# Gate units of the memory branch between its last tile groups, and the heads' sums of squares made by ScalarE, in a hybrid encoder layer on one core

## The chip, the core and the metric

The kernel runs on one core of one Trainium2 chip (trn2). The core has a matrix engine (TensorE, PE in the rows, whose weight loads are listed apart as PEld), a vector engine (VectorE, DVE), a scalar engine for activation functions (ScalarE, ACT), GpSimd (POOL), and SyncE (SP), which here issues all transfers between HBM and on-chip memory. Each engine executes its own instructions in the order in which the program has them, and waits on semaphores for the others. The metric is the device time of one execution in microseconds.

## What is computed

One layer of a streaming encoder, for 1024 prompt rows and 32 sample rows of width 1024, in float32. From the normalised input one projection makes the inputs of three branches: differential attention with 4 heads, a linear recurrence (LRU), and cross-attention into 256 memory tokens with 4 heads of 64. Each branch has a SiLU gate. The gated results are concatenated, projected and added to the input. What the change touches of it:

```python
# memory branch
qm = rms_norm(mq.reshape(B, T, MX_HEADS, MX_HEAD_DIM), p['mx_q_norm_g'])
sm = jnp.einsum('bqhd,bkhd->bhqk', qm, m_k.astype(qm.dtype)).astype(f32) * (MX_HEAD_DIM ** -0.5)
pm = jax.nn.softmax(sm, axis=-1)
om = jnp.einsum('bhqk,bkhd->bqhd', pm.astype(qm.dtype), m_v.astype(qm.dtype)).reshape(B, T, MX_WIDTH)
out_c = om * jax.nn.silu(mg)
# attention branch: every head's output has its own norm
o = rms_norm(o, p['da_subln_g']) * (1.0 - lambda_init)
out_a = o.reshape(B, T, DA_WIDTH) * jax.nn.silu(dg)
y = x + jnp.concatenate([out_a, out_b, out_c], axis=-1) @ p['w_out']
```

## The kernel before

**Precision.** TensorE multiplies in a reduced float32 format (`F32R`). Each operand is split into a high and a low part (`XH`, `XL` of the normalised input, `WH`, `WL` of the weights), and a product is three matmuls (`mm3`, lines 607 to 609: high by high, high by low, low by high). A tile is split by ScalarE, which copies it into the high part, and VectorE, which subtracts (`split`, lines 436 and 438). Weights are split so by `split_all` (lines 591 and 593) into a ring of 4480 columns. A chunk gets its place in the ring only when the unit that last used the old contents there is through (`gone`).

**Units.** The row tiles are 8 of 128 prompt rows and one of 32 sample rows (index 8, `NT`). A unit is one PSUM bank of a projection: `unit_nat` (line 607 and, for the sample rows, 629) makes a row tile by 256 or 384 columns with 24 matmuls (16 for the sample rows), `unit_T` makes 128 features by 352 rows with 24 matmuls of 352 columns. The units of the projections run in the order of `ORDER`: head 0, LRU input, LRU gate, head 1, first half of the attention's gate, memory keys and values (`mk`, `mv`), memory queries with their gate (`mq`, `mg`), heads 2 and 3, second half of the attention's gate (`dg1`), and then the output projection (`wo`) in four blocks of 256 columns.

**The memory branch.** `mem_q` goes through five groups of tiles, four of two full tiles and the sample rows. A tile's unit makes its queries. `mem_probs` norms them, transposes them (L1235), makes the scores in two halves of two heads (L1254, L1256), takes the maximum (DVE, L1260) and the exponential with its sum (ACT, L1263, into `mw`). `mem_pt` divides by the sum (POOL, L1271, `mw`), transposes (PE, L1277), and splits into `PT`; `mem_out` multiplies with the values (L1301). Between groups, `mem_q` puts units of the gate `mg`: there are six (two blocks of 128 features by three blocks of 352 rows), each followed on ACT by a tanh (L971) and on DVE by a product (L972), `silu2`. `paced(mg)` issues one unit if one is left; `unpaced(mg)` issues what is left after the last group.

**The mixing.** The attention's output goes through HBM (`o_d`, with a 129th column per head that carries the epsilon of its norm). For each tile, `mix_T` multiplies the other two branches by their gates (POOL, L1170) and splits them into `XH`, `XL` (rows 4 to 7), and `mix_diff` does the attention's part: load `mn`, square (ACT, L1205), sum per head (DVE, L1206), power -1/2 (POOL, L447, `mrs`), scale (POOL, L1209), transpose (PE, L1214), multiply by gain and gate (DVE, L1215, `mg`), split into rows 0 to 3 of `XH`, `XL`. It can start when the attention of head 2 is done, while head 3's still runs. An output unit multiplies rows 4 to 7 first and then rows 0 to 3 (`ks = [4, 5, 6, 7, 0, 1, 2, 3]`), so its second half waits for `mix_diff`.

**What orders the instructions.** A list scheduler in the file (`Sched`) runs when the kernel is built. The functions above are generators that yield one instruction each, with its engine, a cost and what it depends on; the scheduler always issues the one that can start earliest by those costs, and among those that can start within a window the one of the best priority (`PR`). Nothing is reordered on the chip. A change of any cost or of the order of the units can therefore move instructions on every engine.

Of the kernel before, what the change touches and what calls it, by code (L numbers as in the profile page):

```python
# [9 lines left out]
AF = mybir.ActivationFunctionType  # L10
ALU = mybir.AluOpType
AX = mybir.AxisListType
# [25 lines left out]

PR = {"att": 6, "consts": 37, "evac": 11, "fetch": 1, "fetch0": 11, "gate": 53, "kq": 27, "lru": 13, "lrus": 58, "lrux": 48, "memc": 33, "meme": 47, "memo": 19, "memp": 48, "mempt": 55, "mems": 3, "mixT": 53, "mixd": 22, "normT": 16, "normT0": 34, "out": 16, "outin": 34, "silu": 18, "split": 56, "split0": 56}

TUNE = {"LAG": 0, "O": 3, "PENALTY": 1283, "S": 6, "acc": 3, "aging": 12, "lanes": 3, "tr": 4, "wACT": 455, "wDVE": 94, "wPE": 11, "wPOOL": 54, "F": 1.07, "M": 200, "twice": 127, "LAG2": 3}
LEAST = {"acc": 2, "tr": 1, "S": 2, "O": 1}

PE, ACT, DVE, POOL, SP = "PE", "ACT", "DVE", "POOL", "SP"
# [191 lines left out]
def c_act(n, ap=0, acc=False, sb=False):  # L236
    return (90.0 if sb else 51.0) + 0.833 * n + 93.0 * ap + (93.0 if acc else 0.0)


def c_dve(n, ap=0, fast=False):  # L240
    return 68.0 + (0.52 if fast else 1.042) * n + 60.0 * ap
# [14 lines left out]
def emit(tc, A, Y):  # L256
    nc = tc.nc
    V_, S_, G_, T_, Q_ = nc.vector, nc.scalar, nc.gpsimd, nc.tensor, nc.sync
# [922 lines left out]
    def mix_diff(i):  # L1181
        n, t0 = rows_of(i), i * P
        d = yield WAIT, mix_up
# [9 lines left out]
        g = yield GET, mn_s  # L1193
        mn = mixp.t([P, 4, P + 1], "mn", bufs=2)
        if n < P:
            g = yield from clear(mn, 516, [g])
        d = yield from dma(mn[:n], o_d[t0:t0 + n], od + [g], kb=258)
# [3 lines left out]
        g = yield GET, msq_s  # L1201
        msq = mixp.t([P, 4, P + 1], "msq")
        mss = mixp.t([P, 4], "mss", bufs=2)
        mrs = mixp.t([P, 4], "mrs", bufs=2)
        d = yield ACT, c_act(516, sb=True), [d, g], lambda: S_.activation(out=msq[:n], in_=mn[:n], func=AF.Square)  # L1205
        d = yield DVE, c_dve(516), [d], lambda: V_.tensor_reduce(out=mss[:n], in_=msq[:n], axis=AX.X, op=ALU.add)  # L1206
        msq_s.rel(d)
        d = yield from rsqrt(mrs, mss, n, 4, [d])
        d = yield POOL, c_pool(512), [d], lambda: G_.tensor_tensor(  # L1209
            out=mn[:n, :, :P], in0=mn[:n, :, :P], in1=bcast(mrs[:n], [n, 4, P], 2), op=ALU.mult)  # L1210
        g, (bank,) = yield GET, tr_s
        tr = bank.rearrange("p (k t) -> p k t", k=4)
        for h in range(4):
            t = yield PE, c_pe(128), [d, g], lambda: T_.transpose(tr[:, h, :], mn[:, h, :P], ident)  # L1214
        d = yield DVE, c_dve(4 * n, 1), [t, gd], lambda: V_.scalar_tensor_tensor(  # L1215
            out=gt[:, :, :n], in0=tr[:, :, :n], scalar=gs, in1=gt[:, :, :n], op0=ALU.mult, op1=ALU.mult)
        tr_s.rel(d, bank)
        h, l = mix_dst(i, slice(0, 4))
        d = yield from split(h, l, gt[:, :, :n], 4 * n, [d, xd])
# [142 lines left out]
    def projections():  # L1362
# [71 lines left out]
        def mem_q():  # L1434

            ch = chunks["mq"]
            mg = gates_T("mg", 2)
            yield WAIT, mkv_done
            groups = [[2 * g, 2 * g + 1] for g in range(4)] + [[NT]]
            for gi, tiles in enumerate(groups):  # L1440
                which = "s" if tiles[0] == NT else "p"
                evs = [Event() for _ in range(2 * len(tiles))]
                for j, i in enumerate(tiles):
                    acc, d = yield from unit_nat(ch, i, 0, 256, i == NT)
                    last_x("mq", i, d)
                    sc.spawn(mem_probs(i, acc, d, which, j * P, gi, evs[2 * j:2 * j + 2]), PR["memp"])
                n = NS if tiles[0] == NT else 256
                sc.spawn(mem_out(tiles, which, gi, evs, tiles[0] * P, n), PR["memo"])
                for _ in range(2):
                    yield from paced(mg)  # L1450
            yield from unpaced(mg)

# [67 lines left out]
    for i in range(NT + 1):  # L1520
        n = rows_of(i)
# [75 lines left out]
```

## Time and profile before

| | |
|---|---|
| time, median of 3 runs (lowest, highest) | 582.81 us (581.65, 584.17) |
| the profiled execution: its time, its span | 581.81 us, 580.0 us |
| mean granted clock of TensorE | 0.996 |
| busy share of the span: PE, DVE, ACT, POOL | 95%, 72%, 57%, 46% |
| matmuls on PE | 3840 |
| the chain that ended last: PE, POOL, DVE, issue, ACT, DMA | 75%, 8%, 6%, 5%, 3%, 2% |

All times of the rows below are from one profiled execution; its time includes a little around the span from the first to the last instruction. The busy time of an engine is that of its instructions; matmuls are pipelined, so consecutive ones overlap in the rows, and what one costs is read from the start of one to the start of the next. An instruction's idle time before it stands in brackets, with what ended it. The granted clock is given as a share of 2.4 GHz.

### The profile page before, as it was taken

What the parts mean: (1) busy time and instruction counts of PE and PEld (TensorE: products, weight loads), DVE (VectorE), ACT (ScalarE), POOL (GpSimd) and SP (SyncE); (2) the same over time, 40 slices, a digit from 0 to 9 for tenths busy, and PEclk for the clock granted to TensorE, in tenths of its full rate; (3) what the DMA queues carried; (4) which work ended last, traced back from release to release, by engine and by line L of the source; (5) the groups of instructions that cost most, each with busy time, mean ns of one, the idle gap of its engine ahead of it and who ended that gap; (6) DMA issues with size and microseconds to landing.
All of it is one profiled execution on the core that took longest, in us unless ns stands there. A gap on an engine that the chain in (4) does not pass through costs nothing.

```text
span 580.0 us, 11527 instructions
## 1 busy us (share of the span) xinstructions
PE 552.0 (95%) x3840; PEld 535.2 (92%) x3840; DVE 420.4 (72%) x1018; ACT 332.3 (57%) x863; POOL 268.1 (46%) x477
## 2 busy tenths in 40 slices
PE   3999999999999999999997999999999889999997
PEld 3989999999998999899995999899999889999997
DVE  4877998469468989865569589888798999732421
ACT  5954775765775776765579457646575656310200
POOL 3899732013878413234354577765742553330000
PEclk9999999999999999999999999999999899999999
DMA  8611222112205433320003411311136978452331
GB/s 284 203 57 25 77 68 72 54 60 89 63 2 156 133 108 112 88 72 32 27 32 102 122 38 39 96 46 33 44 115 190 265 226 239 121 139 65 117 96 56
DMA packets 76325, 57.46 MB, mean 99 GB/s; under 512 B 9201, under 2 KB 73514, under 8 KB 76266
## 3 DMA queue, kind: packets, MB, share of 16 engines
q1 hardware_dynamic: 76266, 56.73, 33.1%
q8 instruction: 30, 0.49, 0.4%
q14 instruction: 29, 0.24, 0.1%
HBM read 38.85 MB, written 17.85 MB: 98 GB/s over the span
## 4 chain that ended last, share of the span: by engine, by line
PE 75%; POOL 8%; DVE 6%; issue 5%; ACT 3%; DMA 2%; SPq 1%; POOLq 0%; DVEq 0%; ACTq 0%
PE bank L608 18%; PE bank L607 18%; PE bank L609 18%; PE bank L892 6%; PE bank L880 2%; PE bank L629 2%; PE bank L843 2%; PE bank L842 2%; POOL rs L447 2%; PE bank L1301 1%; PE bank L787 1%; DMA xt<-in_x_prompt 1%; PE bank L1277 1%; POOL nat L487 1%; DVE WL L593 1%
## 5 line engine op out<-in xcount | busy, mean ns | idle before, releaser
L608 PE MATMUL bank<-WL,XH 128*128 128x384 f32 (+1 forms) x512 | 162.1, 317 | 4.1 <-DVE WL L593 4.1
L607 PE MATMUL bank<-WH,XH 128*128 128x384 f32 (+1 forms) x512 | 161.6, 316 | 1.4 <-ACT XH L436 1.4
L609 PE MATMUL bank<-WH,XL 128*128 128x384 f32 (+1 forms) x512 | 161.5, 315 | 0.0
L608 PEld LDWEIGHTS bank<-WL,XH 128*128 128x128 f32 x512 | 97.3, 190 | 5.8 <-DVE WL L593 5.6
L607 PEld LDWEIGHTS bank<-WH,XH 128*128 128x128 f32 x512 | 97.4, 190 | 2.1 <-ACT XH L436 1.8
L609 PEld LDWEIGHTS bank<-WH,XL 128*128 128x128 f32 x512 | 97.4, 190 | 0.6 <-DVE XL L438 0.2
L855 ACT ACTIVATE P<-bank,mx 128x512 f32<-128x512 f32 (+3 forms) x104 | 58.1, 562 | 37.7 <-DVE mx L852 19.1
L609 PE MATMUL bank<-XH,WL 128*128 128x352 f32 x240 | 78.8, 328 | 0.0
L608 PE MATMUL bank<-XL,WH 128*128 128x352 f32 x240 | 78.2, 326 | 0.0
L607 PE MATMUL bank<-XH,WH 128*128 128x352 f32 x240 | 78.2, 326 | 0.0
L447 POOL TENSOR_TENSOR rs<-ss,mhalf 128x4 f32<-128x4 f32 (+1 forms) x47 | 51.6, 1099 | 30.9 <-DVE ss L477 30.7
L849 DVE TENSOR_REDUCE mx<-bank 128x1 f32<-128x512 f32 (+4 forms) x104 | 55.2, 532 | 12.7 <-PE bank L843 10.9
L593 DVE SCALAR_TENSOR_TENSOR WL<-wraw,pcol,WH 128x256 fp32r<-128x256 f32 (+1 forms) x96 | 52.6, 553 | 3.1 <-ACT WH L591 2.8
L591 ACT ACTIVATE WH<-wraw,pcol 128x256 fp32r<-128x256 f32 (+1 forms) x96 | 51.4, 541 | 4.1 <-DMA wraw<-in_w_mem_kv 2.3
L609 PEld LDWEIGHTS bank<-XH,WL 128*128 128x128 f32 x240 | 45.2, 189 | 0.2
L608 PEld LDWEIGHTS bank<-XL,WH 128*128 128x128 f32 x240 | 45.2, 188 | 0.2
L607 PEld LDWEIGHTS bank<-XH,WH 128*128 128x128 f32 x240 | 45.1, 188 | 0.3
L1341 DVE TENSOR_TENSOR on<-bank,on 128x256 f32<-128x256 f32 x32 | 13.5, 422 | 43.4 <-PE bank L609 41.7
L436 ACT ACTIVATE uh<-bank 128x512 fp32r<-128x512 f32 (+4 forms) x52 | 24.2, 468 | 26.1 <-PE bank L880 25.8
L892 PE MATMUL bank<-KV,ul 128*128 128x256 f32 x144 | 37.3, 286 | 1.5 <-DVE ul L438 1.5
L487 POOL TENSOR_TENSOR nat<-nat,bc_in 128x256 f32<-128x256 f32 (+1 forms) x38 | 29.8, 784 | 18.1 <-DVE nat L480 11.7
L892 PE MATMUL bank<-KV,uh 128*128 128x256 f32 x144 | 37.3, 286 | 0.4 <-ACT uh L436 0.4
(256 smaller groups left out, 1350.5 us busy)
## 6 DMA issues: line engine op xcount, KB each, us to landing
wraw<-in_w_in SPq DMA_DIRECT2D x32, 192.0 KB, 2.6
wraw<-in_w_in SPq DMA_DIRECT2D x48, 128.0 KB, 2.1
gt_d<-nat SPq DMA_DIRECT2D x24, 176.0 KB, 1.9
xt<-in_x_prompt SPq DMA_DIRECT2D x8, 512.0 KB, 4.3
wraw<-in_w_out SPq DMA_DIRECT2D x32, 128.0 KB, 2.8
on<-in_x_prompt SPq DMA_DIRECT2D x32, 128.0 KB, 2.8
out_yp<-on SPq DMA_DIRECT2D x32, 128.0 KB, 1.9
o_d<-OP SPq DMA_DIRECT2D x32, 64.5 KB, 1.9
```

The source lines that it names most:

```text
L436: d = yield ACT, c_act(n), deps, lambda: S_.activation(out=h, in_=src, func=AF.Copy)
L447: d = yield POOL, c_pow(k), deps, lambda: G_.tensor_tensor(out=rs[:n], in0=ss[:n], in1=mhalf[:n].to_broadcast([n, k]), op=ALU.pow)
L487: d = yield POOL, c_pool(w), [ds], lambda: G_.tensor_tensor(out=d3, in0=d3, in1=gain, op=ALU.mult)
L591: d = yield ACT, c_act(n, 1, sb=True), [dd, g, dp, du], lambda: S_.activation(out=h, in_=raw[:, :n], func=AF.Copy, scale=scale(k))
L593: d = yield DVE, c_dve(n, 1), [d], lambda: V_.scalar_tensor_tensor(out=l, in0=raw[:, :n], scalar=scale(k), in1=h.bitcast(F32), op0=ALU.mul ...
L607: yield PE, c_pe(n), deps, lambda: T_.matmul(out, ah, bh, start=first, stop=False)
L608: yield PE, c_pe(n), deps, lambda: T_.matmul(out, ah, bl, start=False, stop=False)
L609: d = yield PE, c_pe(n), deps, lambda: T_.matmul(out, al, bh, start=False, stop=last)
L849: d = yield DVE, c_dve(ln), [d, gm], lambda: V_.tensor_reduce(out=mx[:n, c, s:s + 1], in_=S[:n], axis=AX.X, op=ALU.max, negate=True)
L855: e = yield ACT, c_act(ln, 1, True), [d, gP], lambda: S_.activation(out=Pc[c][:n, k0:k0 + ln], in_=St[s][:n], func=AF.Exp, bias=mx[:n, c, ...
L892: t = yield PE, c_pe(256, n), [e, gO, vd], lambda: T_.matmul(O[:n].rearrange("p s e -> p (s e)"), u[:, b - b0, :n], V[:, b].rearrange("p s ...
L1341: d = yield DVE, c_dve(256), [d, e], lambda: V_.tensor_tensor(out=xr[:n], in0=acc[:n, :256], in1=xr[:n], op=ALU.add)
```

## The change

Two edits. In `mem_q` the number of gate units behind each group of tiles comes from a table: none behind the first two groups, one behind the third, two behind the fourth, three behind the sample rows (before: two behind each group until the six are used). In `mix_diff` the one square of 516 columns on ScalarE and VectorE's sum over them are replaced by four squares of 129 columns, one per head, that also write the sum (`accum_out`).

```diff
-TUNE = {..., "LAG2": 3}
+TUNE = {..., "LAG2": 3, "mg0": 0, "mg1": 0, "mg2": 1, "mg3": 2, "mg4": 3}
...
-        d = yield ACT, c_act(516, sb=True), [d, g], lambda: S_.activation(out=msq[:n], in_=mn[:n], func=AF.Square)
-        d = yield DVE, c_dve(516), [d], lambda: V_.tensor_reduce(out=mss[:n], in_=msq[:n], axis=AX.X, op=ALU.add)
+        dl = d
+        for h in range(4):
+            d = yield ACT, c_act(129, 0, True, True), [dl, g], lambda: S_.activation(
+                out=msq[:n, h], in_=mn[:n, h], func=AF.Square, accum_out=mss[:n, h:h + 1])
         msq_s.rel(d)
...
-                for _ in range(2):
+                for _ in range(TUNE[f"mg{gi}"]):
                     yield from paced(mg)
```

Lines behind the squares are numbered two higher in the changed kernel. PE's order is the same up to the first unit of the memory queries' gate, again from the middle of head 2 to the head of the mixing, and again from the last output units of the first three blocks to the end.

The first place is PE at the end of the memory stage. Before, head 2's first unit (128x384) begins right behind the sample rows' unit (L629) and the scores of one full tile:

```order
L1254 MATMUL bank_73<-MKV,QAm 128x256
L1256 MATMUL bank_73<-MKV,QLm 128x256
L607 MATMUL bank_71<-WH,XH 128x384
L608 MATMUL bank_71<-WL,XH 128x384
L609 MATMUL bank_71<-WH,XL 128x384
```

In the change the sample rows' unit is followed by the first of three gate units (128x352):

```order
L629 MATMUL bank_75<-WH,XS 64x256
L629 MATMUL bank_75<-WL,XS 64x256
L607 MATMUL bank_70<-XH,WH 128x352
L608 MATMUL bank_70<-XL,WH 128x352
L609 MATMUL bank_70<-XH,WL 128x352
```

Head 2's first unit comes three gate units later than the sample rows' unit; the scores and transposes of the last tiles now lie between the gates' matmuls.

The second place is PE at the head of the mixing. Before, the transposes of tile 0 (L1214) and tile 1 have four score matmuls of head 3 (L842, L843) and four transposes (L880) between them, and then the second half of the first output unit (`bank_70`) goes on:

```order
L1214 MATMUL bank_73<-ident,mn 128x128 x4
L842 MATMUL bank_71<-KV,QA 128x512
L843 MATMUL bank_71<-KV,QLleft 128x512
L842 MATMUL bank_68<-KV,QA 128x256
L843 MATMUL bank_68<-KV,QLleft 128x256
L880 MATMUL bank_72<-ident,P_5835 128x128 x4
L1214 MATMUL bank_75<-ident,mn 128x128 x4
L607 MATMUL bank_70<-WH,XH 128x256
```

In the change (L1216 is L1214 of before) the transposes of tile 1 follow eight products with V and one transpose, and four transposes, two products with V and four score matmuls come ahead of the second half of the first output unit (`bank_68`):

```order
L880 MATMUL bank_74<-ident,P_5835 128x128
L1216 MATMUL bank_75<-ident,mn 128x128 x4
L880 MATMUL bank_71<-ident,P_5934 128x128 x4
L892 MATMUL bank_73<-KV,uh 128x256
L892 MATMUL bank_73<-KV,ul 128x256
L842 MATMUL bank_69<-KV,QA 128x512
L843 MATMUL bank_69<-KV,QLleft 128x512
L842 MATMUL bank_72<-KV,QA 128x384
L843 MATMUL bank_72<-KV,QLleft 128x384
L607 MATMUL bank_68<-WH,XH 128x256
```

Ten products with V, five transposes and four score matmuls moved in front of that half.

The third place is VectorE at the same time. Before, the product with gain and gate of tile 0 (`mg`, L1215) is followed closely by the low part of that tile (`XL<-mg`):

```order
L1215 SCALAR_TENSOR_TENSOR mg<-bank_73,gs,mg 128x512
L849 TENSOR_REDUCE mx<-bank_71 128x1
L972 SCALAR_TENSOR_TENSOR nat<-nat,bank_69 128x352
L848 MEMSET bank_68 64x64
L593 SCALAR_TENSOR_TENSOR WL<-wraw,half,WH 128x256
L438 TENSOR_TENSOR XL<-mg,XH 128x4x128
```

In the change the product of tile 0 stands just ahead of this piece, and tile 0's `XL<-mg` ends it:

```order
L438 TENSOR_TENSOR ul<-bank_71,uh 128x512
L972 SCALAR_TENSOR_TENSOR nat<-nat,bank_72 128x352
L593 SCALAR_TENSOR_TENSOR WL<-wraw,half,WH 128x256
L861 TENSOR_TENSOR sm<-sm 128x2
L867 RECIPROCAL cf<-sm 128x1
L868 SCALAR_TENSOR_TENSOR cf<-cf,neglam,sm 128x1
L870 SCALAR_TENSOR_TENSOR P_5934<-P_6013,cf,P_5934 128x768
L593 SCALAR_TENSOR_TENSOR WL<-wraw,half,WH 128x256
L438 TENSOR_TENSOR XL<-bt,XH 128x4x128
L1217 SCALAR_TENSOR_TENSOR mg<-bank_75,gs,mg 128x512
L438 TENSOR_TENSOR ul<-bank_74,uh 128x128
L438 TENSOR_TENSOR XL<-mg,XH 128x4x128
```

Between the two there were four instructions and are now eleven, among them `P` of head 3's next tile, one more weight split, and the gate product of tile 1. ScalarE's rows there changed too: its squares of tile 1 stand behind the exponentials that they stood ahead of.

## Rows read from the trace of the kernel before

**Rows 1.** The page: busy us (share of the span) and instructions of each engine.
```profile
PE 552.0 (95%) x3840; PEld 535.2 (92%) x3840; DVE 420.4 (72%) x1018; ACT 332.3 (57%) x863; POOL 268.1 (46%) x477
```

**Rows 2.** Windows by stage: length, busy us (count) by engine, TensorE clock, DMA share, GB/s.
```profile
250.00:300.00 50.00, 50.00 (x384) 49.94 (x383) 28.52 (x66) 28.87 (x87) 20.88 (x26) 1.00 0.13 41
300.00:320.00 20.00, 15.73 (x109) 13.63 (x108) 18.02 (x39) 18.23 (x51) 10.56 (x14) 1.00 0.26 79
320.00:440.00 120.00, 119.51 (x770) 115.27 (x769) 98.23 (x279) 72.91 (x220) 76.13 (x147) 1.00 0.24 69
456.00:470.00 14.00, 10.04 (x64) 9.18 (x64) 12.59 (x26) 7.93 (x18) 6.67 (x7) 0.88 0.88 253
470.00:500.00 30.00, 30.00 (x248) 29.54 (x248) 27.79 (x64) 15.88 (x40) 14.61 (x16) 1.00 0.70 206
500.00:580.00 80.00, 76.62 (x650) 76.39 (x648) 24.68 (x56) 10.08 (x23) 6.59 (x7) 0.99 0.33 97
```

**Rows 3.** Timeline, TensorE, memory stage: start us, us, instruction [idle before it <- releaser].
```profile
310.54 0.66 PE L1277 MATMUL bank<-ident,mw 128*128 128x128 f32 x4 [1.23 <-POOL mw L1271]
...
318.02 0.66 PE L1277 MATMUL bank<-ident,mw 128*128 128x128 f32 x4 [1.33 <-POOL mw L1271]
```

**Rows 4.** Timeline of TensorE in the mixing: its three waits.
```profile
456.32 0.66 PE L880 MATMUL bank<-ident,P 128*128 128x128 f32 x4 [0.24 <-DVE P L870]
...
458.67 0.66 PE L1214 MATMUL bank<-ident,mn 128*128 128x128 f32 x4 [1.69 <-POOL mn L1209]
...
469.72 0.39 PE L608 MATMUL bank<-WL,XH 128*128 128x256 f32 x1 [2.03 <-DVE WL L593]
```

**Rows 5.** Timeline of TensorE: two matmuls of a gate unit, three others between them.
```profile
273.28 0.32 PE L607 MATMUL bank<-XH,WH 128*128 128x352 f32 x1
...
274.07 0.32 PE L609 MATMUL bank<-XH,WL 128*128 128x352 f32 x1
```

**Rows 6.** Timeline of TensorE: first score matmul (L1254) and transposes of probabilities (L1277).
```profile
276.73 0.36 PE L1254 MATMUL bank<-MKV,QAm 128*128 128x256 f32 x1
...
282.56 0.60 PE L1277 MATMUL bank<-ident,mw 128*128 128x128 f32 x4
...
303.97 0.36 PE L1254 MATMUL bank<-MKV,QAm 128*128 128x256 f32 x1
...
310.95 0.36 PE L1254 MATMUL bank<-MKV,QAm 128*128 128x256 f32 x1
```

**Rows 7.** Groups by line, 250 to 300 us: ... xcount | busy us, mean ns | idle before.
```profile
L971 ACT ACTIVATE nat<-bank 128x352 f32<-128x352 f32 x6 | 2.8, 464 | 2.9 <-PE bank L609 2.8
...
L972 DVE SCALAR_TENSOR_TENSOR nat<-nat,bank 128x352 f32<-128x352 f32 x6 | 3.1, 520 | 3.0 <-ACT nat L971 2.9
```

**Rows 8.** Timeline of VectorE at the head of the mixing.
```profile
448.76 0.68 DVE L438 TENSOR_TENSOR XL<-bt,XH 128x512 fp32r<-128x512 f32 x1
...
450.59 0.68 DVE L1206 TENSOR_REDUCE mss<-msq 128x4 f32<-128x516 f32 x1
451.19 0.68 DVE L849 TENSOR_REDUCE mx<-bank 128x1 f32<-128x512 f32 x1
...
458.82 0.68 DVE L438 TENSOR_TENSOR XL<-mg,XH 128x512 fp32r<-128x512 f32 x1
...
469.19 0.47 DVE L593 SCALAR_TENSOR_TENSOR WL<-wraw,half,WH 128x256 fp32r<-128x256 f32 x1
```

**Rows 9.** Timeline of ScalarE at the head of the mixing.
```profile
449.07 0.64 ACT L1205 ACTIVATE msq<-mn 128x516 f32<-128x516 f32 x1
449.61 0.69 ACT L855 ACTIVATE P<-bank,mx 128x512 f32<-128x512 f32 x1
...
450.28 0.36 ACT L855 ACTIVATE P<-bank,mx 128x128 f32<-128x128 f32 x1
...
450.62 0.50 ACT L591 ACTIVATE WH<-wraw,half 128x256 fp32r<-128x256 f32 x1
```

**Rows 10.** Timeline of GpSimd at the head of the mixing.
```profile
455.03 1.34 POOL L447 TENSOR_TENSOR mrs<-mss,mhalf 128x4 f32<-128x4 f32 x1 [1.30 <-DVE mss L1206]
456.35 1.26 POOL L1170 TENSOR_TENSOR bt<-bt,gt 128x512 f32<-128x512 f32 x1
```

More of the change, by code (lines that the diff above doesn't have):

```diff
@@ L39 @@
 PR = {"att": 6, "consts": 37, "evac": 11, "fetch": 1, "fetch0": 11, "gate": 53, "kq": 27, "lru": 13, "lrus": 58, "lrux": 48, "memc": 33, "meme": 47, "memo": 19, "memp": 48, "mempt": 55, "mems": 3, "mixT": 53, "mixd": 22, "normT": 16, "normT0": 34, "out": 16, "outin": 34, "silu": 18, "split": 56, "split0": 56}
-TUNE = {"LAG": 0, "O": 3, "PENALTY": 1283, "S": 6, "acc": 3, "aging": 12, "lanes": 3, "tr": 4, "wACT": 455, "wDVE": 94, "wPE": 11, "wPOOL": 54, "F": 1.07, "M": 200, "twice": 127, "LAG2": 3}
+TUNE = {"LAG": 0, "O": 3, "PENALTY": 1283, "S": 6, "acc": 3, "aging": 12, "lanes": 3, "tr": 4, "wACT": 455, "wDVE": 94, "wPE": 11, "wPOOL": 54, "F": 1.07, "M": 200, "twice": 127, "LAG2": 3, "mg0": 0, "mg1": 0, "mg2": 1, "mg3": 2, "mg4": 3}
 LEAST = {"acc": 2, "tr": 1, "S": 2, "O": 1}
```

## The prediction

> **What bounds the kernel now.** I read the busy totals first. TensorE (PE) is busy 95% of the span, VectorE (DVE) 72%, ScalarE (ACT) 57%, GpSimd (POOL) 46% [rows 1]. Such a kernel can only win where PE stands still, so I went next to the windows by stage and took PE's busy time from each length [rows 2]. In 250 to 300 us PE never stops. In 300 to 320, the end of the memory cross-attention, it is busy 15.73 of 20.00 us: 4.27 us lost, while DVE (18.02) and ACT (18.23) are nine tenths busy. From 320 to 440 it loses 0.49, from 456 to 470, the head of the mixing and of the output projection, 3.96, from 470 to 500 nothing. The 3.38 us lost in 500 to 580 are the drain after the last matmul. The two places that the change touches are the two with loss.
>
> Third, PE's own rows with the idle time before them. In the memory stage PE waits 1.23 and 1.33 us for the transposes of the normalised probabilities, released by POOL's product into `mw` [rows 3]; the rest of the 4.27 are shorter waits for head 2's split weights. I read it so: after the last memory tile only head 2 is left for PE, its weights are being split just then on ACT and DVE, and the softmax of the last tiles needs the same two engines. In the mixing PE waits 0.24 us for `P`, 1.69 for POOL's `mn`, and 2.03 for the last `WL` of the second column block [rows 4]. There the granted clock also falls: its mean over the 14 us is 0.88 [rows 2], which means that PE ran part of them at 1.2 GHz, not 2.4. 0.12 x 14 = 1.7 us of work is lost beside the idle 3.96, 5.66 in all.
>
> **Part one: the gate units.** No matmul is added or removed. A gate unit is 24 matmuls of 352 columns. Five of them take 274.07 - 273.28 = 0.79 us [rows 5], 0.158 each, so a unit is 3.8 us of PE. Before, two units stood after each of the first three tile groups; now one after the third, two after the fourth, three after the sample rows. Five units, 19 us, leave the front for the end, into a stretch that lacked 4.27. PE's work in 250 to 320, 65.73 us, stays, so the ceiling of the gain is 4.27.
>
> How much of it is reached? What matters is the PE work between a tile's score matmuls and the transposes that read its softmax. In the front one such pair starts at 276.73 and 282.56, 5.83 us apart, without a wait; the pairs 303.97 to 310.54 and 310.95 to 318.02 are those that waited, though 6.6 and 7.1 us passed [rows 3, 6]. So a pair needs at most 5.8 us in the front, and up to 7 where ACT and DVE are full. Counting matmuls in the order (0.119 us for 256 columns, 0.158 for 352, 0.07 for a transpose: starts to starts in PE's timeline), the first ten pairs of before had 4.8 to 7.2 us of PE work between them, the two that waited 3.6 and 4.1. In the change the sixteen pairs of full tiles have 4.9 to 8.8, three of them under 5.6. Most of head 2's weights also get three units, 11 us, between the release of their ring space and their first use, where there was nothing.
>
> Against it: the front gets denser. A unit costs ACT a tanh of 0.46 and DVE a product of 0.52 us [rows 7]. Without five units the front has 50.0 - 19.0 = 31.0 us of PE work for 28.87 - 2.3 = 26.6 of ACT and 28.52 - 2.6 = 25.9 of DVE, 86% and 84%, if all of it had to be done there. Part of it trails into the filled end, yet three tight pairs at some 0.4 us each are likely. I take 1.2 us of new idle time: **-3.1 us** (bounds -4.27, and -2.0 if the tight pairs wait half as long as those seen).
>
> **Part two: the squares.** Nine tiles are mixed. DVE loses nine sums `mss`; the next instruction starts 0.60 us after one (450.59 to 451.19) [rows 8], so 5.4 us leave DVE. ACT's square of 516 took 0.54 (449.07 to 449.61). A square of 129 with an accumulator is not in the trace; the nearest row is the exp of 128 columns with its accumulator, 450.28 to the next instruction at 450.62, 0.34 us [rows 9]. The exp has a bias column and reads PSUM, the square has none and reads SBUF, so I bound it by 0.25 and 0.45 and take 0.34: 4 x 0.34 - 0.54 = +0.82 us a tile, +7.4 in all (+4.1 to +11.3). In 456 to 500 ACT has 23.8 us of work in 44 [rows 2]; even with all 7.4 there it is 71% busy, while DVE had 40.4 and gets 35. Neither sum is on PE's path by itself. The Trainium skill (ScalarE: Activation LUTs, section Rules for kernel authors) speaks against this edit: multiplications belong on VectorE. By that rule alone the edit loses 7.4 - 5.4 = 2.0 us of engine time; the rows show that the engine that pays is the one with room.
>
> What decides is when DVE, which works in order, reaches two results. (a) `XL<-mg` of tile 0, which lets the second half of the first output unit start. Before, it is the 24th DVE instruction from the first `XL<-bt` on, 9.3 us by durations; it ended at 458.82 + 0.68 = 459.5, 10.7 us after 448.76 [rows 8], so 1.4 us were waits. In the change it is the 33rd, 12.5 us by durations: 461.3 without waits, 462.7 with the same, 463.3 if they grow. PE has more to do ahead of it: what it had done by 456.3, then ten products with V (1.2 us), nine transposes (0.6) and four score matmuls (0.9), to 459.0. So it idles 2.3 to 4.3 us there, against 3.96 in the whole stage before. (b) The last `WL` of the second block, 469.19 on DVE, for which PE waited 2.03: by durations it comes 1.0 us earlier (15.9 for 16.9), and PE has 3.7 us more work ahead of it, so this wait goes. POOL's `mrs` of tile 1 comes about 0.3 us later, but its `mn` product now follows directly and not behind a `bt` product of 1.26 us [rows 10]: 1.0 us earlier. I take 3.4 us idle and half of the clock's loss, 0.9: 4.3 against 5.66, **-1.3 us** (bounds: 2.3 without a fall of the clock, -3.4; 4.3 with the fall as before, +0.3).
>
> **Sum.** The profiled execution took 581.81 us around its span of 580.0. 581.81 - 3.1 - 1.3 = 577.4. The median of the three runs, 582.81, is 1.0 above that execution, so I forecast **578.4**. A difference under 0.5%, 2.9 us, is about what a measurement of this kernel cannot tell from none.
>
> **Rivals.** First, only the gates help: the first output unit waits the full 4.3 us for `XL<-mg` and the clock falls as before. 581.81 - 3.1 + 0.3 = 579.0, median 580.0. For it: 33 instructions on an engine that is 12.59 of 14.00 us busy. Against: wait (b) goes in any case. Chance 0.24.
>
> Second, on the other side: the stall moves to the front. With ACT at 58% in 250 to 300 PE lost nothing, at 91% in 300 to 320 it lost 21%. At 86% a line between them gives 18%, 5.6 us of the 31.0: +1.3 instead of -3.1. With +0.3 in the mixing that is 583.4, median 584.4, and 586.1 if the clock falls there as it did in the mixing. It decides if PE waits more than 4.3 us for `mw`, `qn` or `QAm` ahead of the sample rows. For it: the front's load. Against: the distances, none under 4.9. Chance 0.12.
>
> Third, both stalls vanish: 581.81 - 4.27 - 5.66 = 571.9, median 572.9. For it: PE has other work at both places. Against: (a). Chance 0.10.
>
> **How the numbers follow.** The forecast keeps 0.54; with its bounds it spans 575.1 to 581.1 as a median. The range goes on to 574.0, towards the third case, and to 584.0, nearly the second. Faster by over 0.5%, under 579.9: nine tenths of the forecast, the third case, and a little of the first: 0.60. Slower, above 585.7: most of the second case: 0.09. Within: 0.31.
>
> **What would show it.** Right: no wait for `mw` or `WL` over 0.5 us between the last full memory tile and head 2's second unit; about 1 us of PE idle in the memory stage; squares 0.34 us apart; the 2.03 us wait for `WL` gone, and 2 to 4 us of idle PE around the products with V and the second half of the first output unit. Wrong: more than 2 us idle ahead of the sample rows, more than 4.3 us in the mixing, or a clock below 0.85 over its first 14 us.

## The result, and the profile after

The changed kernel took 574.15 us (median of 4 runs, 573.59 to 574.26) against 582.51 (581.65 to 584.17) for the kernel before in the same comparison: a ratio of 0.9849, 95% interval 0.9826 to 0.9873, 8.4 us. The forecast was 578.4, a gain of 4.4 against the median of 582.81 known then. The profiled execution took 573.59 us around a span of 571.8.

The busy totals of the page (before: [rows 1]):

```profile
PE 549.7 (96%) x3840; PEld 535.1 (94%) x3840; DVE 415.5 (73%) x1009; ACT 336.8 (59%) x925; POOL 268.3 (47%) x478
```

VectorE lost 4.9 us and ScalarE gained 4.5, both in the direction of the edit (the prediction had 5.4 and 7.4). The windows by stage, columns as in [rows 2]:

```profile
250.00:300.00 50.00, 50.00 (x389) 49.78 (x388) 35.75 (x84) 35.28 (x106) 26.29 (x32) 1.00 0.15 47
300.00:320.00 20.00, 20.00 (x138) 19.87 (x138) 15.50 (x33) 13.98 (x40) 10.11 (x16) 1.00 0.39 118
...
440.00:456.00 16.00, 13.08 (x91) 12.09 (x90) 14.94 (x37) 14.23 (x49) 8.94 (x9) 1.00 0.87 255
456.00:470.00 14.00, 13.89 (x106) 13.33 (x107) 13.97 (x30) 9.28 (x34) 8.90 (x8) 1.00 0.93 266
```

In the memory stage PE no longer stops, and no new idle time stands in the front, where DVE and ACT are busy 72% and 71% (250 to 300 us). At the head of the mixing, now some 6 us earlier, it loses 2.92 + 0.11 = 3.03 us where it lost 3.96, and the granted clock stays at 1.00 (it was 0.88 over 14 us). PE's waits there, from its timeline (`uh` and `ul` are the high and the low part of the transposed probabilities `P`):

```profile
451.61 0.39 PE L892 MATMUL bank<-KV,ul 128*128 128x256 f32 x1 [1.07 <-DVE ul L438]
454.03 0.66 PE L880 MATMUL bank<-ident,P 128*128 128x128 f32 x4 [0.78 <-DVE P L870]
455.89 0.38 PE L892 MATMUL bank<-KV,ul 128*128 128x256 f32 x1 [1.08 <-DVE ul L438]
```

The waits for `mn` (1.69) and `WL` (2.03) of [rows 4] are gone; three others, of about 1 us, stand at the products with V and the transposes.

**Where the 8.2 us of span come from** is read from the same instruction in both kernels. VectorE's rows, first of the kernel before:

```profile
205.88 0.42 DVE L899 TENSOR_REDUCE OP<-bank 128x128 f32<-128x256 f32 x1 [0.31 <-PE bank L892]
...
447.95 0.69 DVE L438 TENSOR_TENSOR ul<-bank,uh 128x512 fp32r<-128x512 f32 x1
```

and of the changed kernel:

```profile
206.80 0.42 DVE L899 TENSOR_REDUCE OP<-bank 128x128 f32<-128x256 f32 x1 [0.31 <-PE bank L892]
...
441.68 0.69 DVE L438 TENSOR_TENSOR ul<-bank,uh 128x512 fp32r<-128x512 f32 x1
```

Ahead of the gates the changed kernel is 0.92 us late (its start, which differs a little between executions), at the head of the mixing 6.27 early, at the end 8.2. So the memory stage gave 7.2 us and the mixing 2.0 in these two executions. From the mixing's windows went 3.96 - 3.03 = 0.9 us of idle time and 0.12 x 14 = 1.7 of clock, somewhat more than the 2.0, and most of it is the clock that did not fall. The memory stage's 7.2 are far more than the 4.27 that its windows had to give. PE's timeline of the kernel before says why:

```profile
249.37 0.30 PE L892 MATMUL bank<-Vs,ul 128*32 128x256 f32 x1 [0.43 <-DVE ul L438]
...
308.22 1.09 PE L1301 MATMUL bank<-PT,MKV 128*128 128x256 f32 x8
...
312.03 1.11 PE L1301 MATMUL bank<-PT,MKV 128*128 128x256 f32 x8
312.98 0.33 PE L607 MATMUL bank<-WH,XH 128*128 128x384 f32 x1
```

The eight products at 312.03 are followed by the next matmul 0.95 us later. Those at 308.22 are followed by the wait for `mw` of [rows 3], at 310.54, 2.32 us later: 1.37 lost, 1.23 printed. A matmul of 352 columns is listed with 0.32 us and starts 0.158 after the one before it [rows 5], so a wait is printed short by the tail of the listed time that otherwise overlaps. The first matmuls after a wait are also spaced wider: the four transposes at 318.02 take 0.41 for a usual 0.35, and the matmul behind them 0.28 for 0.175. Summed over every step between starts in 300 to 320 us, each less the usual step of its kind (0.175 us for 384 columns, 0.12 for 256, 0.07 to 0.09 for a transpose), the kernel before loses about 6.8 us, the changed one 0.3 to 0.6, by the step taken as usual for a transpose. With the wait at 249.37, 0.59 from start to start, which went too, that is about the 7.1 or 7.2 by which the instructions shifted.

The window itself had a nearer figure beside PE's: its second busy column, the weight loads, shows 13.63 of 20.00 us in 300 to 320 before [rows 2], so 6.37 missing, and 19.87 in the change.

The Trainium skill (TensorE: Matmul & The Clock Gate, Single matmul latency) has a formula for a lone bf16 matmul at 2.4 GHz, by which 256 columns would take an estimated (398 + 256) / 2.4 = 272 ns. The trace, in another format, lists 0.28 us for a matmul of the product with V at 249.52, with 0.12 us from start to start. It agrees as far as a listed time can tell, since the profile models the ends of matmuls.

On ScalarE the squares stand 0.295 us apart, where 0.34 was taken:

```profile
445.03 0.30 ACT L1207 ACTIVATE msq<-mn 128x129 f32<-128x129 f32 x1
445.23 0.20 ACT L1207 ACTIVATION_READ_ACCUMULATOR msq<-mn 128x1 f32 x1
445.32 0.30 ACT L1207 ACTIVATE msq<-mn 128x129 f32<-128x129 f32 x1
```

### The profile page after: what moved, and what is told of

Read it like the earlier page. It is cut to its first block, busy times and chain, and to the rows that moved or that the text cites. A ratio compares the mean times of both kernels' runs of the same rounds, so it can differ in the third digit from the quotient of the medians.

```text
span 571.8 us, 11596 instructions
## 1 busy us (share of the span) xinstructions
PE 549.7 (96%) x3840; PEld 535.1 (94%) x3840; DVE 415.5 (73%) x1009; ACT 336.8 (59%) x925; POOL 268.3 (47%) x478
## 4 chain that ended last, share of the span: by engine, by line
PE 80%; DVE 7%; POOL 6%; issue 4%; DMA 2%; ACT 1%; SPq 1%; POOLq 0%; DVEq 0%; ACTq 0%
PE bank L607 19%; PE bank L608 19%; PE bank L609 19%; PE bank L892 5%; PE bank L629 3%; PE bank L843 3%; PE bank L880 2%; PE bank L842 2%; PE bank L1303 2%; PE bank L1279 1%; PE bank L787 1%; DMA xt<-in_x_prompt 1%; DVE mx L849 1%; POOL rs L447 1%; POOL nat L487 1%
```

## The experiments

All runs in one table. The last two columns are from the profiled executions: by how much earlier the same PE matmuls start than in the kernel before, gained between 60 and 430 us (the memory stage), and from there to the end. They belong to one execution each, and hold what TensorE's clock did in it.

| kernel | time, us | ratio to before (95%) | memory stage | mixing to end |
|---|---|---|---|---|
| the change | 574.15 | 0.9849 (0.9826 to 0.9873) | 7.2 | 2.0 |
| 1 gates only | 574.86 | 0.9867 (0.9841 to 0.9892) | 7.1 | -0.1 |
| 2 squares only | 586.08 | 1.0056 (1.0035 to 1.0076) | -1.6 | -2.2 |
| 3 order of the change, old sums | 576.32 | 0.9898 (0.9874 to 0.9922) | 7.1 | -3.8 |
| 4 gates moved, old mixing order, new squares | 573.20 | 0.9834 (0.9811 to 0.9856) | 7.2 | 2.5 |
| 5 as 2, `mn` on ACT | 584.58 | 1.0045 (1.0030 to 1.0061) | 0.0 | -1.2 |
| 6 as 2, no POOL product | 585.88 | 1.0062 (1.0043 to 1.0081) | -0.1 | -2.7 |
| 7 as 4, `mn` on ACT | 573.14 | 0.9842 (0.9825 to 0.9858) | 7.1 | 2.3 |
| 8 as 4, no POOL product | 574.11 | 0.9862 (0.9842 to 0.9881) | 7.1 | 0.4 |
| 9 gates 2, 2, 1, 1, 0 | 591.34 | one run | | |
| 10 gates 2, 2, 0, 0, 2 | 592.83 | one run | | |
| 11 gates 1, 1, 1, 1, 2 | 579.48 | 0.9951 (0.9934 to 0.9968) | | |
| 12 as 4, `XL<-bt` on POOL | 576.18 | 0.9892 (0.9872 to 0.9912) | 7.1 | -1.3 |
| 13 the change, no POOL product | 577.66 | 0.9916 (0.9897 to 0.9936) | 7.1 | -2.6 |
| 14 as 4, POOL products in quarters | 573.52 | 0.9845 (0.9818 to 0.9873) | 7.2 | 1.7 |
| 15 as 4, POOL products in halves | 572.82 | 0.9836 (0.9814 to 0.9858) | 7.1 | 2.2 |

**Runs 1 and 2: each edit alone.** Run 1 has the old square and sum:

```diff
-        dl = d
-        for h in range(4):
-            d = yield ACT, ..., func=AF.Square, accum_out=mss[:n, h:h + 1])
+        d = yield ACT, c_act(516, sb=True), [d, g], lambda: S_.activation(out=msq[:n], in_=mn[:n], func=AF.Square)
+        d = yield DVE, c_dve(516), [d], lambda: V_.tensor_reduce(out=mss[:n], in_=msq[:n], axis=AX.X, op=ALU.add)
```

> The gate units moved as in the change, the squares and their sum as before. Theory A: a wait costs PE more than the idle time printed beside it. From the start of the matmul ahead of a wait to the start of the one behind it, less what that step takes without a wait, the seven waits between 305 and 320 us of the kernel before lose about 6.5 us, where the windows show 4.27 us idle; all of it goes. Then this kernel takes 6.3 to 7 us less than before: about 576, and its span up to the head of the mixing is shorter by about 7 us. Rival: only the printed idle time of 4.27 us can be won, and the rest of the 8.4 us comes from the squares: about 578.2.

Measured 574.86, 7.5 us less than before, somewhat over theory A's 6.3 to 7; in the profiled execution 7.1 us in the memory stage and nothing in the mixing, whose waits are those of the kernel before (1.69 for `mn`, 2.04 for `WL`). Theory A holds: the stage had 7 us to give, not 4.27. By the medians little is left for the squares: the change is 0.7 us faster than this run, and their intervals overlap, so beside the new gates the squares are not shown to gain. In the profiled execution of run 1 the clock fell behind the wait for `mn` (mean 0.83 in 450 to 460), as before; three others of its six have a mean clock of 0.999 or 1.000 and took 573.64 to 574.64, about the time of the change.

Run 2 has the old gates:

```diff
-TUNE = {..., "mg0": 0, "mg1": 0, "mg2": 1, "mg3": 2, "mg4": 3}
+TUNE = {..., "mg0": 2, "mg1": 2, "mg2": 2, "mg3": 0, "mg4": 0}
```

> The squares with accumulators on ScalarE as in the change, the gate units two behind each group as before. Theory A: the memory stage keeps its waits, and the mixing alone gains about 2 us: 580.5. Rival (the gates give only 4.27): the squares give the other 4 us: about 578.5. If the two edits need each other (the mixing's order depends on where the gates end), neither number holds and the two gains don't add up to 8.4.

Neither number holds: alone the squares make the kernel slower, by 0.35 to 0.76%. All engines have the order of the change from within head 2 on, and yet PE waits longer there:

```profile
462.34 0.39 PE L892 MATMUL bank<-KV,ul 128*128 128x256 f32 x1 [2.99 <-DVE ul L438]
464.75 0.66 PE L880 MATMUL bank<-ident,P 128*128 128x128 f32 x4 [0.76 <-DVE P L870]
467.68 0.49 PE L892 MATMUL bank<-KV,ul 128*128 128x256 f32 x1 [2.16 <-DVE ul L438]
```

These are the three waits of the change, two of them longer by 1.92 and 1.08 us. Behind the third the clock falls as well (mean 0.96 over 440 to 480 us, 1.00 in the change). Runs 5, 6 and 13 look for the reason of the waits.

**Runs 3 and 4: work or order?** The order of the change with the old work, and the old order with the new work. Each `yield` hands the scheduler one instruction with its cost; run 3 keeps the four of the squares, and with them the order, but fills them with the old work:

```diff
+            def sums(h=h):
+                if h == 0:
+                    S_.activation(out=msq[:n], in_=mn[:n], func=AF.Square)
+                if h == 3:
+                    V_.tensor_reduce(out=mss[:n], in_=msq[:n], axis=AX.X, op=ALU.add)
+            d = yield ACT, c_act(129, 0, True, True), [dl, g], sums
```

> The instruction order of the changed kernel on every engine, but in the place of each tile's first square ScalarE makes the one square of 516 columns, the other three squares are left out, and VectorE makes the sum in the place of the fourth. VectorE has 9 sums of 0.60 us more than the changed kernel. Theory B: the mixing gains because the order makes short waits out of two long ones, not because VectorE has less to do: 574.2, at most 0.6 more for the one sum that lies ahead of the first output unit's second half. Rival C: VectorE's 5.4 us less are the gain: the mixing's 2 us come back, about 576.2.

Run 4 keeps the two yields of before and fills them with the four squares:

```diff
+        def squares():
+            for h in range(4):
+                S_.activation(out=msq[:n, h], in_=mn[:n, h], func=AF.Square, accum_out=mss[:n, h:h + 1])
+        d = yield ACT, c_act(516, sb=True), [d, g], squares
+        d = yield DVE, c_dve(516), [d], lambda: None
```

> The gate units as in the change, and the order of the kernel before in the mixing, but in the place of each square of 516 columns ScalarE makes the four squares with accumulators, and VectorE's sum is left out. Theory B: with the old order the two long waits in the mixing stay, shorter by 0.6 to 1.2 us at most: 575 to 576, nearly the kernel with the gates alone. Rival C: VectorE's 5.4 us less are the gain whatever the order: 574.2.

Theory B falls; rival C holds for run 3 (576.2) and is the nearer one for run 4 (574.2). With the new order the sums cost 576.32 - 574.15 = 2.2 us (the intervals touch no more, 0.9874 and 0.9873); with the old order 574.86 - 573.20 = 1.7 (their intervals overlap). The new order itself costs 1.0 to 1.5 us, by medians whose intervals overlap. In run 4 the old waits for `mn` and `WL` are there, but 0.89 for 1.69 and 1.31 for 2.03, and the clock stays at 1.00:

```profile
450.15 0.66 PE L1217 MATMUL bank<-ident,mn 128*128 128x128 f32 x4 [0.89 <-POOL mn L1212]
456.48 0.66 PE L880 MATMUL bank<-ident,P 128*128 128x128 f32 x4 [0.78 <-DVE P L870]
459.96 0.39 PE L608 MATMUL bank<-WL,XH 128*128 128x256 f32 x1 [1.31 <-DVE WL L593]
```

In run 3 the waits for `ul` are 1.97 and 1.60, and behind them PE ran at 1.2 GHz (its window 456 to 460, in slices of 4 us, columns as above):

```profile
456.00:460.00 4.00, 2.81 (x10) 2.62 (x11) 4.00 (x9) 1.57 (x4) 0.00 (x0) 0.50 0.69 188
```

That execution was the slowest of its six, 2.3 us over their median, so the -3.8 of the table is too much for run 3 at large. Its time goes with the clock: the two executions at a mean of 0.990 took 578.66 and 578.26, the four at 0.994 to 0.997 took 575.49 to 576.45. Part of what the sums cost, in this order, is the clock behind longer waits.

**Runs 5 and 6: where VectorE meets POOL.** In run 2, VectorE's rows from 456 to 467 and POOL's:

```profile
456.05 1.53 DVE L438 TENSOR_TENSOR XL<-bt,XH 128x512 fp32r<-128x512 f32 x1
457.50 1.52 DVE L593 SCALAR_TENSOR_TENSOR WL<-wraw,half,WH 128x256 fp32r<-128x256 f32 x1
...
460.24 0.79 DVE L852 TENSOR_TENSOR mx<-mx 128x1 f32<-128x1 f32 x1
...
465.00 1.76 DVE L438 TENSOR_TENSOR XL<-bt,XH 128x512 fp32r<-128x512 f32 x1
```

```profile
455.97 1.06 POOL L1211 TENSOR_TENSOR mn<-mn,mrs 128x512 f32<-128x512 f32 x1
457.46 1.28 POOL L1170 TENSOR_TENSOR bt<-bt,gt 128x512 f32<-128x512 f32 x1 [0.43 <-DMA gt<-gt_d]
...
459.98 1.04 POOL L1211 TENSOR_TENSOR mn<-mn,mrs 128x512 f32<-128x512 f32 x1
...
464.80 1.42 POOL L1170 TENSOR_TENSOR bt<-bt,gt 128x512 f32<-128x512 f32 x1 [1.30 <-DMA gt<-gt_d]
```

Each long VectorE instruction begins inside a POOL product and ends only behind that product's end: the first `XL` at 457.58 behind 457.03, the last at 466.76 behind 466.22. The first one began 0.08 us later than POOL. The same pair of `XL` and `mn` in the changed kernel, VectorE 0.26 us early:

```profile
447.02 0.68 DVE L438 TENSOR_TENSOR XL<-bt,XH 128x512 fp32r<-128x512 f32 x1
447.62 1.26 DVE L593 SCALAR_TENSOR_TENSOR WL<-wraw,half,WH 128x256 fp32r<-128x256 f32 x1
```

```profile
447.28 1.32 POOL L1211 TENSOR_TENSOR mn<-mn,mrs 128x512 f32<-128x512 f32 x1
```

There `XL` has its 0.68, and POOL and the `WL` behind it wait. Ahead of the first wait VectorE loses 0.85 + 1.04 + 0.63 = 2.5 us in run 2 and 0.8 in the change: 1.7 of the 1.92 by which that wait differs. The 1.08 of the last `XL<-bt` is the difference of the third. The kernel before has such a row too, ahead of its 2.03 us wait for `WL`: an `XL<-bt` of 1.78 us at 466.56. The Trainium skill (SBUF — State Buffer, section SBUF: two separate sides) says that a VectorE operation with two inputs in SBUF and a GpSimd operation that reads SBUF lock a shared pair of ports, and that the one that starts first has it for its whole instruction; the trace agrees in the rows above, and in the change `nat<-nat,bank` at 451.47, which has one operand in PSUM, keeps its 0.51 inside POOL's product of 451.08 to 452.12.

Run 5 takes one product from POOL, run 6 both (first the edit of both runs, then what run 6 has beside it):

```diff
-        d = yield POOL, c_pool(512), [d], lambda: G_.tensor_tensor(
-            out=mn[:n, :, :P], in0=mn[:n, :, :P], in1=bcast(mrs[:n], [n, 4, P], 2), op=ALU.mult)
+        def scaled():
+            for h in range(4):
+                S_.activation(out=mn[:n, h, :P], in_=mn[:n, h, :P], func=AF.Copy, scale=mrs[:n, h:h + 1])
+        d = yield POOL, c_pool(512), [d], scaled
```

> The kernel with the squares alone (586.1), but the product mn*mrs of the mixing is made by ScalarE, four instructions of 128 columns with a scale, in POOL's place in the order. Theory D: in the mixing VectorE stands still where an instruction of its own with two operands in SBUF meets a POOL product: in the squares-only kernel XL<-bt at 456.05 took 1.53 us for 0.68 and mx at 460.24 took 0.79 for 0.16, both over a product mn of POOL. Without that product 0.85 + 0.63 us go ahead of the first wait for ul, which falls from 2.99 to about 1.5 us, and the kernel takes 584 to 585. Rival E: the long instructions have another cause (transfers, the place of the gates), and nothing changes: 586, or more for ScalarE's extra 1.2 us a tile.

```diff
-        d = yield POOL, c_pool(4 * n), [d1, d2], lambda: G_.tensor_tensor(out=bt[:, :, :n], in0=bt[:, :, :n],
+        d = yield POOL, c_pool(4 * n), [d1, d2], lambda: V_.tensor_tensor(out=bt[:, :, :n], in0=bt[:, :, :n],
...
```

> As the run before, and the product bt*gt of the mixing is made by VectorE in POOL's place in the order, so POOL has no product of 512 columns left in the mixing; VectorE has 9 more of about 0.65 us. Theory D: no instruction of VectorE in the mixing takes over 1.1 us any more; 0.85 + 1.04 + 0.63 + 1.08 us of blocked time go in the first 15 us, and 1.3 come for two products: the first wait for ul falls to 1 to 1.5 us, and the kernel takes 582 to 585. Rival E: 586 plus 0.65 for each product ahead of a wait: 587 to 588.

Run 5 came at 584.58, in theory D's range, though its interval overlaps that of run 2, and 1.6 us of the difference between the two profiled executions is the memory stage's clock (last section). The rows lengthened over `mn` are gone. The first wait for `ul` is 0.41 us, but one of 0.55 for `uh` on ScalarE, now fuller, is new, and the wait for `P` grew from 0.76 to 1.82. In run 6 no VectorE instruction between 440 and 480 us takes over 1.1 us; its time, 585.88, lies between the two theories. The meetings are shown; taking them away by loading ACT and VectorE does not pay.

**Run 13: the test.** The edits of run 6 in the changed kernel.

> The changed kernel with the products mn*mrs on ScalarE and bt*gt on VectorE, each in POOL's place in the order, as in the run of the squares alone without POOL products, which lost 2.7 us in the mixing against the kernel before. The order of both is the same from head 2 on. Theory D (the two kernels differ by where VectorE and POOL meet): without POOL products their mixings are alike, this one loses 2 to 3 us there as well and takes 582.2 - 7.1 + 2.7 = about 577.5 to 578. Rival I (something that comes with the gates' places, as when the transfers of the mixing start, makes the difference): this mixing still gains, 574 to 575.

577.66, inside theory D's half microsecond. Without POOL's products the mixing comes out the same with the gates before and after, -2.7 and -2.6 us, where with them it was -2.2 and +2.0. But the two sums are made of different terms. The windows from 440 to 480 us, in turn of run 2, the change, run 6 and run 13:

```profile
440.00:480.00 40.00, 34.09 (x228) 32.34 (x227) 37.19 (x80) 24.19 (x84) 16.35 (x16) 0.96 0.79 225
440.00:480.00 40.00, 36.96 (x277) 35.24 (x276) 38.41 (x86) 29.59 (x102) 21.59 (x20) 1.00 0.89 252
440.00:480.00 40.00, 34.85 (x227) 33.05 (x226) 33.95 (x84) 27.51 (x95) 4.75 (x7) 0.91 0.79 226
440.00:480.00 40.00, 35.94 (x238) 33.76 (x237) 34.48 (x82) 30.80 (x103) 5.27 (x7) 0.87 0.78 222
```

With POOL's products PE is idle 5.91 us beside the old gates and 3.04 beside the new, 2.87 apart; without them 5.15 and 4.06, 1.09 apart. So about 1.8 of the 2.9 us of waits go with POOL's products. The clock makes the rest: it is lower in run 2 than in the change, and in run 13 it is lower than in run 6, which hides the 1.09. `XL<-bt` in runs 6 and 13 has its usual time:

```profile
455.10 0.68 DVE L438 TENSOR_TENSOR XL<-bt,XH 128x512 fp32r<-128x512 f32 x1
```

```profile
447.32 0.68 DVE L438 TENSOR_TENSOR XL<-bt,XH 128x512 fp32r<-128x512 f32 x1
```

So who came first at POOL's products made most of the difference in waits between the change and the squares alone. The clock added some 1.6 us; it fell behind the longer waits, but that their length made it fall is not shown. That run 13 hit theory D's number is in part luck. Why the phase shifts by some tenths of a microsecond was not settled; two of the POOL products above began when a transfer of `gt` landed, so the transfers are a candidate that no run tested.

**Runs 7 and 8: the same on run 4.** The edits of runs 5 and 6.

> The kernel with the gates moved, the old order in the mixing and ScalarE's squares (573.2), with the product mn*mrs on ScalarE as well. Its VectorE rows show WL at 444.55 taking 1.35 us for 0.48 over POOL's product mn, and XL<-bt at 461.15 taking 1.32 for 0.68. Theory D: that time comes back, about 1 us on PE's path: 572 to 572.7. Rival F: the transposes wait longer for mn, since ScalarE is at 14 of 16 us busy from 440 to 456 and has 1.2 us a tile more: 574 or more.

> As the run before, and the product bt*gt on VectorE in POOL's place. Theory D: 0.96 + 0.80 us more of blocked VectorE time go (cf at 454.34, WL at 458.47), but three products of 0.65 us come ahead of the last long wait: no gain over the run before, 572 to 573.5. Rival F: VectorE is the bound of this stage, busy 15.5 of 16 us, and 9 products more cost what the 9 sums cost: 575 to 577.

573.14 and 574.11: no gain over run 4. The last wait for `WL` fell from 1.31 to 1.03 in run 7, but the transposes now wait 0.97 for ScalarE's `mn`. In run 8 the clock falls too (0.88 in 456 to 470). Both lie between their theories.

**Runs 9 to 11: other places for the gates**, on run 4, each a change of the table's five numbers only:

```diff
-TUNE = {..., "mg0": 0, "mg1": 0, "mg2": 1, "mg3": 2, "mg4": 3}
+TUNE = {..., "mg0": 2, "mg1": 2, "mg2": 1, "mg3": 1, "mg4": 0}
```

> The kernel with the old order of the mixing and ScalarE's squares (573.2), gate units 2, 2, 1, 1, 0 behind the five groups: one unit, 3.8 us of PE work, behind the fourth group and none behind the sample rows. Theory A (the stall is a lack of PE work, 6.5 us long from start to start): 2.5 to 4 us of the loss in the memory stage go and 3 to 4 stay, the time is 576 to 577. Rival G (what decides is the distance of each pair of scores and transposes, and only units between them help): the two waits for mw stay whole, at 1.2 to 1.3 us each, and the time is 579 or more. The orders of heads 2 and 3 change a little with it, so only the memory stage is read.

> As the run before, gate units 2, 2, 0, 0, 2: two units, 7.6 us of PE work, behind the sample rows, where the waits are. Theory A: 7.6 us are enough for a loss of 6.5, so under 1 us of idle PE stays in the memory stage: 573 to 574.5. Rival G: the front before it has the pairs of the change at its end, without units between, and waits for mw come back ahead of the sample rows: over 2 us of idle time, 576 or more.

> As the two runs before, gate units 1, 1, 1, 1, 2, spread over all groups. Theory A: three units lie where there was none, 11.4 us: no idle time over 0.5 us in the memory stage, and the time is that of the change's table, 573 to 574. Rival H (the front was near its limit, as the prediction took it): the change's table is worse than this one, and the spread units win 1 us more: 572.

In run 9 PE is idle 4.39 us in 300 to 320, about as before: one unit ahead of the sample rows does not fill the stall, and the two waits for `mw` stay nearly whole, as rival G has it:

```profile
310.20 0.66 PE L1280 MATMUL bank<-ident,mw 128*128 128x128 f32 x4 [1.22 <-POOL mw L1274]
...
317.82 0.66 PE L1280 MATMUL bank<-ident,mw 128*128 128x128 f32 x4 [1.08 <-POOL mw L1274]
```

In run 10, two units behind the sample rows, PE is busy without a gap from 250 to 320, as theory A has it, and so is it in run 11 but for 0.30 us. Their times are far off theory A all the same, as is that of run 9. With any of these tables the scheduler also writes another order of heads 2 and 3, and there the time is lost, in run 10 most of all, where PE is idle 10.10 us between 340 and 380 and the mean clock is 0.79:

```profile
376.48 1.12 PE L880 MATMUL bank<-ident,P 128*128 128x128 f32 x4 [4.42 <-DVE P L870]
```

and in run 11 at the mixing (2.27 us for `mn` at 461.34). The change's table is spared that: PE's order is again that of before from the middle of head 2.

**Run 12: less VectorE work still.** Run 4 with `XL<-bt` made by POOL in VectorE's place in the order:

```diff
-        d = yield from split(h, l, bt[:, :, :n], 4 * n, [d, xd])
+        src = bt[:, :, :n]
+        d = yield ACT, c_act(4 * n), [d, xd], lambda: S_.activation(out=h, in_=src, func=AF.Copy)
+        d = yield DVE, c_dve(4 * n), [d], lambda: G_.tensor_tensor(out=l, in0=src, in1=h.bitcast(F32), op=ALU.subtract)
```

> The old order of the mixing and ScalarE's squares (573.2), with the low parts of the LRU half, XL<-bt, made by POOL in VectorE's place in the order: VectorE has 9 instructions of 0.60 us less, POOL 9 of about 1.26 more. Theory C (VectorE's work on the way is what the mixing's waits hang on): another 1 to 2 us go, 571.2 to 572.2. Rival D (POOL's longer stretches hold up VectorE's own instructions with two operands in SBUF): each of POOL's products costs VectorE up to 1.1 us, nothing is won: 573 to 575.

576.18, more than either said: PE waits 1.48 and 2.06 us for POOL's `mn` (0.89 in run 4). The clock falls as well (0.83 in 460 to 470). Neither theory had counted POOL's own queue.

**Runs 14 and 15: shorter POOL products.** On run 4, POOL's one product made in quarters (`h:h + 1`), then halves (`h:h + 2`), for `mn` and likewise for `bt`:

```diff
+            for h in range(0, 4, 1):
+                G_.tensor_tensor(out=mn[:n, h:h + 1, :P], in0=mn[:n, h:h + 1, :P],
+                                 in1=bcast(mrs[:n, h:h + 1], [n, 1, P], 2), op=ALU.mult)
```

> The kernel with the old order of the mixing and ScalarE's squares (573.2), with each product of 512 columns of POOL in the mixing (mn*mrs, bt*gt) made as four of 128. Theory D: VectorE waits for the product that is running, so for at most a quarter: cf at 454.34 (1.03 us for 0.22), WL at 458.47 (1.44 for 0.48) and XL<-bt at 461.15 (1.32 for 0.68) come down by about 0.6 each, and 0.5 to 1.2 us are won: 572 to 572.7. Rival J (POOL's next quarter goes ahead of the waiting VectorE instruction): VectorE waits for all four, which take longer together than the one: 573.5 to 575.

> As the run before, in two products of 256. Theory D: half of the gain of the quarters, with less time lost in starting instructions on POOL: 572.4 to 573. Rival J: 573.3 to 574.

573.52 and 572.82, not to be told from run 4. The first is rival J's number, but not by its mechanism: VectorE gets in between quarters:

```profile
455.95 0.22 DVE L868 SCALAR_TENSOR_TENSOR cf<-cf,neglam,sm 128x1 f32<-128x1 f32 x1
...
459.27 0.47 DVE L593 SCALAR_TENSOR_TENSOR WL<-wraw,half,WH 128x256 fp32r<-128x256 f32 x1
```

where run 4 had 1.03 and 1.44, and the waits for `P` and `WL` fell from 0.78 and 1.31 to 0.25 and 0.34. But POOL's product takes longer:

```profile
444.92 2.17 POOL L1216 TENSOR_TENSOR mn<-mn,mrs 128x128 f32<-128x128 f32 x4
```

for 1.03 in one piece. Two of its quarters took 0.39 us and two 0.58 and 0.91, among VectorE's instructions, which now go ahead of them (an `XL<-bt` from 445.79 to 446.47). The transposes wait 0.69 + 0.21 + 0.48 for `mn` instead of 0.89. Runs 4, 7 and 15 have the lowest medians, 573.2 to 572.8; their intervals overlap that of the change, so none is shown to beat it.

## Why the prediction came out too small

**The memory stage** was forecast at -3.1 us and gave 7.2. The step that failed is the term "so the ceiling of the gain is 4.27": it took the idle time of the windows for what the waits cost, though it counted the cost of a gate unit from start to start. So counted, the waits cost about 6.8 us in 300 to 320, and 0.59 more stood at 249.37; run 1 shows that 7.1 us could be had. The second mis-sized term is the "1.2 us of new idle time": there is none. (Its bound of -2.0 does not follow either: three pairs at half of 1.23 to 1.33 us make 1.9, which leaves -2.35.) The step behind it, that PE work between a tile's scores and its transposes covers the softmax, held: no pair waits, and the front's DVE and ACT rose to 72 and 71%, not 84 to 86, since part of their work trailed into the filled end. That one unit behind the fourth group does not do it, run 9 shows; which of the units behind the fourth group and the sample rows are needed was not taken apart.

**The squares.** ScalarE's 0.34 us measured 0.295. `XL<-mg` of tile 0 came where step (a) put it, as the 33rd instruction: 455.75 + 0.90 - 442.49 = 14.2 us after the first `XL<-bt`, forecast 12.5 to 14.5. But no matmul waited for it: the three waits are for `ul` and `P`, which stand ahead of it on VectorE, and when PE comes to the second half of the first output unit at 456.92, `XL<-mg` has been done since 456.65. So the 3.03 us of idle time, forecast as 3.4, is near by another path than (a) priced. The waits for `WL` and `mn` went as (b) said, and the clock did not fall, where half of the old loss, 0.9 us, was booked as a middle between two cases. So -2.0 by position for -1.3, and most of the -2.0 is the clock; by the medians of run 1 and the change it is 0.7, not to be told from nothing. What the text missed is how the 5.4 us off VectorE work: runs 3 and 4 put them at 2.2 and 1.7 us by medians, the first with intervals that just part and the second with intervals that overlap, and the new order at a small cost that is not shown. It also took VectorE's durations as fixed. They are not: beside the old gates the same edit lost 3.7 us. The rule of the Trainium skill weighed there, VectorE for multiplications, would have cost 2.0 us by engine time; beside the new gates the edit lost nothing.

**The rivals.** The third, both stalls vanish at 572.9, came nearest to the time, though part of the mixing's stall stays. The first fell with the mixing, where the clock stayed up, the second with a front without idle time. The way from the profiled execution to the median was taken as +1.0 us and was 0.6 in the change.

## To carry to other kernels

Measure a stall on TensorE from the start of one matmul to the start of the next, less the usual step, and check it on the shift of an instruction that stands behind it in both kernels: the printed idle time, 4.27 + 0.43 us, was two thirds of what the stall cost (in this window the weight loads' missing 6.37 us came closer). Where VectorE is nearly full and POOL works beside it, tenths of a microsecond decide who waits for whom: the same edit lost 3.7 us beside the old gates and nothing beside the new, so test it in the place where it will stand. When two runs agree, look at their waits and their clock apart before calling them the same. With a scheduler, read each stage apart, since a table that fills one stall can write a worse order for the next.

## What was not expected of the hardware

TensorE's clock differed after the same waits. In the memory stage of run 2, with the order and the waits of the kernel before (1.22 and 1.33 us for `mw`), the clock fell behind the last of them, as its window shows, and PE came 1.6 us later; in the kernel before it stayed at 1.00 [rows 2], and in run 5 too.

```profile
320.00:360.00 40.00, 39.66 (x245) 38.63 (x244) 28.56 (x80) 21.19 (x67) 27.41 (x50) 0.96 0.25 70
```

In the mixing it fell behind waits of 1.69 us (before, run 1), 1.97 (run 3) and 1.30 and 0.34 close together (run 13), and not behind 1.08 (the change) or 1.31 (run 4), but neither behind the 2.03 at 469.72 of the kernel before [rows 4], after which it stayed at 1.00, nor behind the 2.99 at 462.34 of run 2, where it fell only behind the 2.16 at 467.68. The length of a wait alone does not tell; what else matters was not settled.
